# Two of the four weight sums of a pair by adding DMAs instead of VectorE adds

## The chip, the cores and the metric

One core of one Trainium2 chip. The metric is the device time of one execution in microseconds. The text names engines as the profile does: PE is TensorE's matmul queue (PEld its weight loads), DVE is VectorE, ACT is ScalarE, POOL is GpSimd, SP is SyncE.

## The reference

One inference step of a two-layer decoder trunk, on 512 prompt tokens and 8 sample tokens together (T = 520 columns), width 1024, all in float32:

- layer 0: RMSNorm, then retention (4 heads, in chunks of 128) beside a gMLP gating unit (4 groups), one input projection and one output projection
- layer 1: RMSNorm, then a convolution module (gated projection, causal depthwise convolution of width 31, LayerNorm, swish, projection)
- after each: `x = x + square(relu(rmsnorm(x) @ w1)) @ w2` with a hidden width of 4096
- a final RMSNorm; the recurrent and convolution states are outputs too

The change is in the product `rmsnorm(x) @ w1` of both layers.

## The kernel before

Activations lie feature by token: a tile of 128 features has 520 columns, in two halves of 260. A weight unit (1024 rows by 128 output columns) is loaded by `load_w` (line 124, SyncE's queue) as a tile `raw` of 128 x 8 x 128, 512 KB, of which there are four. To keep float32 accuracy, `split` (lines 132 and 133) turns each half unit into a rounded part `wh` (ScalarE) and a rest `wl` (VectorE subtract); there are five such pairs of tiles. Each product is then three matmuls per 128 x 128 block: high by high, low activation by high weight, high activation by low weight.

The first feed-forward product is computed with a seven-product scheme of Strassen's kind (class `Pair`). A pair is two weight units `t` and `b`, each of two halves: `a11`, `a12` from `t`, `a21`, `a22` from `b`. Four sums of halves are formed, each 128 x 512 numbers, 256 KB:

- s1 = a21 + a22 (line 232), s2 = s1 + a11 (line 233), s4 = s2 + a12 (line 234), s3 = a11 + a21 (line 235)

All four are VectorE adds into four tiles of the tag `wsum`. The seven products use a11, a12, s4, a22, s1, s2, s3; each splits its weight and runs 12 matmuls (line 245). `run` calls the products in the order 1, then the product 4 left over from the pair before, then 2, 5, 6, 3, 7; s1 is the weight of product 5, s2 of 6, s4 of 3, s3 of 7. The activations' side of the scheme is prepared by `Tokens.sums` (lines 203 to 214).

The two layers have 29 pairs: in each, 16 double units of `w1`, of which one (layer 0) or two (layer 1) are computed plainly. `ffn` has four blocks; pairs of a block alternate with "down" units, which multiply by `w2`:

```python
            for i in range(KH):
                up(0, i)
            for blk in range(1, 4):
                up(blk, 0)
                down(blk - 1, 0)
                up(blk, 1)
                ...
```

A down unit is 48 matmuls (line 161, tile `y`). Before the first feed-forward stage stands the output projection (tile `ops`), whose sums go into `x` (line 805) and through `Norm.chunk` (lines 357 and 358; its squares are summed by GpSimd, line 374). At the kernel's very start the eight chunks of the input are loaded (SyncE, lines 405 and 410), turned into `n0h` and `n0l` (line 357, 358) and multiplied with the first weight units.

The instructions' order on each engine is not the program's: the kernel is built with `schedule_with_timeline_sim=True`, by a planner that simulates a timeline at build time and lets each engine issue what is ready, earlier lines first. Each engine then works through its queue in order; a tile of a tag can be written when the one that had its place before is released.

Of the kernel before, what the change touches and what calls it, by code (L numbers as in the profile page):

```python
# [6 lines left out]
F32 = mybir.dt.float32  # L7
# [3 lines left out]
ALU = mybir.AluOpType  # L11
# [3 lines left out]
P = 128  # L15
D = 1024
# [60 lines left out]
def trunk_kernel(tc, a, o):  # L77
    nc = tc.nc
    te, ve, se, pe_ = nc.tensor, nc.vector, nc.scalar, nc.gpsimd
    with ExitStack() as st:  # L80
        cp = st.enter_context(tc.tile_pool(name="const", bufs=1))
        big = st.enter_context(tc.tile_pool(name="big", bufs=5))
        wp = st.enter_context(tc.tile_pool(name="w", bufs=3))
# [7 lines left out]
        def open_stage(name):  # L91
            stage.close()
            return stage.enter_context(tc.tile_pool(name=name, bufs=2, reuse_waits="tile"))

        mp = open_stage("mix0")
# [10 lines left out]
        def aux(name):  # L106
            self_n[0] ^= 1
            return ps.tile([P, 512], F32, name=name, tag="auxA" if self_n[0] else "auxB", bufs=2)
# [13 lines left out]
        def load_w(ap, row, col):  # L122
            raw = wp.tile([P, C, P], F32, name="raw", tag="raw", bufs=RAWS)
            nc.sync.dma_start(raw, ap[row // D, col // P])
            return raw

        KH = C // 2
# [93 lines left out]
        class Pair:  # L221
# [5 lines left out]
            def load(self):  # L227
                ap, row, cols = self.src
                t, b = [load_w(ap, row, c) for c in cols]
                a11, a12, a21, a22 = t[:, :KH], t[:, KH:], b[:, :KH], b[:, KH:]  # L230
                s1, s2, s3, s4 = [wp.tile([P, KH, P], F32, name=f"S{i}", tag="wsum", bufs=4) for i in range(4)]
                ve.tensor_add(s1, a21, a22)
                ve.tensor_add(s2, s1, a11)
                ve.tensor_add(s4, s2, a12)
                ve.tensor_add(s3, a11, a21)
                self.w = {1: a11, 2: a12, 3: s4, 4: a22, 5: s1, 6: s2, 7: s3}
                self.banks = [aux("p" + n)[:, :HALF] for n in "pqr"]

# [557 lines left out]
        mp = open_stage("ffn0")  # L796
# [136 lines left out]
        mp = open_stage("mix1")  # L933
# [4 lines left out]
        for c in range(CFULL, C):  # L938
            tag, bufs, parts = (("s0", 3, 1), ("s0", 3, 1), ("s0", 3, 1), ("S", 1, 1))[c - CFULL]
# [175 lines left out]
        mp = open_stage("ffn1")  # L1115
# [72 lines left out]
```

## Time and profile before

| | |
|---|---|
| median of 3 runs | 1317.53 us (1316.22 to 1317.74) |
| profiled execution | 1319.12 us, span 1317.4 us |
| busy: PE / DVE / ACT / POOL | 1273.5 / 923.0 / 648.7 / 242.7 us |
| mean granted clock of TensorE | 0.985 |
| moved by DMA | 149.21 MB, mean 113 GB/s |
| first feed-forward product and down units of layer 0 | about 399 to 752 us |
| of layer 1 | about 943 to 1304 us |

Busy time is the sum of an engine's instructions; a matmul of 260 columns takes 283 ns from start to end in it, but the next one starts before it ends. A row of a group gives line, engine, operation, output tile and inputs, count, busy time, and the idle time before it with what ended it. A row of the timeline gives start, duration, engine, line and tiles. The clock is 1.00 at full speed.

### The profile page before, as it was taken

The numbers are of one execution on the slowest core, as the hardware profiler recorded it, in microseconds if no ns is written. First come the engines' busy times: TensorE is split into PE (matmuls) and PEld (weight loads), VectorE is DVE, ScalarE is ACT, GpSimd is POOL, SyncE is SP. The second block draws the span as 40 slices with busy tenths as digits, with TensorE's granted clock in tenths as the row PEclk, the third lists the DMA queues.
The fourth block names the chain that finished last, engine by engine and source line by source line (L and its number), as shares of the span: only waits on it lengthen the run. The fifth ranks groups of instructions, "written<-read, shape, count | busy, mean of one in ns | idle before, by whom it ended". The sixth has DMA issues, their size and how long they took to land.

```text
span 1317.4 us, 26073 instructions
## 1 busy us (share of the span) xinstructions
PE 1273.5 (97%) x10618; PEld 1241.4 (94%) x10618; DVE 923.0 (70%) x1634; ACT 648.7 (49%) x1160; POOL 242.7 (18%) x226
## 2 busy tenths in 40 slices
PE   9999999799999999999999999989989999999996
PEld 8999999799998999999999998858989999999995
DVE  6833668965688866766755699968997667676544
ACT  7432343433356643544444476547756445454342
POOL 0521013640020000000000469842200000000012
PEclk9999999899999999999999999999989999999998
DMA  7323235773222323332322322453523333332321
GB/s 281 97 86 104 85 130 193 249 278 111 81 82 81 99 94 97 97 113 81 114 96 96 93 85 81 140 129 112 161 65 97 103 90 101 109 97 81 97 81 65
DMA packets 50407, 149.21 MB, mean 113 GB/s; under 512 B 6112, under 2 KB 13280, under 8 KB 50288
## 3 DMA queue, kind: packets, MB, share of 16 engines
q1 hardware_dynamic: 45888, 134.11, 33.1%
q0 software_dynamic: 3456, 12.58, 2.7%
q8 instruction: 83, 1.36, 0.4%
q10 hardware_dynamic: 944, 0.86, 0.2%
q14 instruction: 36, 0.29, 0.1%
HBM read 139.35 MB, written 9.13 MB: 113 GB/s over the span
## 4 chain that ended last, share of the span: by engine, by line
PE 85%; DVE 9%; issue 2%; ACT 2%; DMA 1%; DVEq 0%; SPq 0%
PE y L161 27%; PE in L161 15%; PE pp L245 12%; PE pq L245 6%; PE ci L161 4%; PE ops L161 3%; PE pr L245 3%; PE f L161 3%; PE opr L161 3%; DVE wl L133 2%; PE co L178 2%; DVE cv L1023 2%; PE cvB L993 1%; PE opr L178 1%; ACT wh L132 0%
## 5 line engine op out<-in xcount | busy, mean ns | idle before, releaser
L132 ACT ACTIVATE wh<-raw 128x512 fp32r<-128x512 f32 x403 | 252.3, 629 | 347.2 <-PE in L161 101.9
L133 DVE TENSOR_TENSOR wl<-raw,wh 128x512 fp32r<-128x512 f32 x403 | 301.0, 749 | 165.8 <-ACT wh L132 159.0
L161 PE MATMUL y<-f,wh 128*128 128x260 f32 x2016 | 323.9, 283 | 0.8 <-DVE x L872 0.8
L161 PEld LDWEIGHTS y<-f,wh 128*128 128x128 f32 x2016 | 275.8, 188 | 1.2 <-DVE x L872 1.2
L161 PE MATMUL y<-f,wl 128*128 128x260 f32 x1008 | 202.6, 282 | 0.0
L161 PEld LDWEIGHTS y<-f,wl 128*128 128x128 f32 x1008 | 155.3, 188 | 0.0
L161 PE MATMUL in<-n0h,wh 128*128 128x260 f32 x640 | 133.0, 287 | 1.2 <-DVE k L470 0.8
L161 PE MATMUL in<-n0l,wh 128*128 128x260 f32 x640 | 130.8, 285 | 1.2 <-DVE n0l L358 1.0
L161 PE MATMUL in<-n0h,wl 128*128 128x260 f32 x640 | 129.6, 284 | 0.1
L132 ACT ACTIVATE wh<-S 128x512 fp32r<-128x512 f32 x116 | 73.1, 631 | 91.4 <-PE y L161 45.5
L133 DVE TENSOR_TENSOR wl<-S,wh 128x512 fp32r<-128x512 f32 x116 | 79.3, 687 | 49.6 <-ACT wh L132 48.4
L161 PEld LDWEIGHTS in<-n0h,wh 128*128 128x128 f32 x640 | 99.0, 188 | 3.6 <-PE in L161 1.3
L161 PEld LDWEIGHTS in<-n0l,wh 128*128 128x128 f32 x640 | 98.7, 188 | 2.7 <-DVE n0l L358 2.5
L245 PE MATMUL pp<-Th,wh 128*128 128x260 f32 x348 | 98.3, 283 | 0.9 <-ACT Th L213 0.9
L161 PEld LDWEIGHTS in<-n0h,wl 128*128 128x128 f32 x640 | 98.6, 188 | 0.4 <-DVE wl L133 0.3
L245 PE MATMUL pp<-Tl,wh 128*128 128x260 f32 x348 | 98.1, 282 | 0.0
L245 PE MATMUL pp<-Th,wl 128*128 128x260 f32 x348 | 97.8, 282 | 0.0
L1016 POOL TENSOR_TENSOR pacc<-pacc,pp 128x512 f32<-128x512 f32 x60 | 88.1, 1478 | 4.5 <-ACT pp L1015 1.7
L374 POOL TENSOR_TENSOR n2acc<-n2acc,n2sq 128x520 f32<-128x520 f32 x5 | 7.0, 1402 | 344.9 <-DVE n2l L358 327.3
L374 POOL TENSOR_TENSOR n4acc<-n4acc,n4sq 128x520 f32<-128x520 f32 x5 | 6.5, 1307 | 346.7 <-ACT n4sq L371 346.7
L245 PEld LDWEIGHTS pp<-Th,wh 128*128 128x128 f32 x348 | 65.5, 189 | 1.4 <-ACT Th L213 1.1
L245 PEld LDWEIGHTS pp<-Tl,wh 128*128 128x128 f32 x348 | 65.5, 188 | 0.0
(406 smaller groups left out, 2919.2 us busy)
## 6 DMA issues: line engine op xcount, KB each, us to landing
raw<-in_ffn_w SPq DMA_DIRECT2D x128, 512.0 KB, 3.6
raw<-in_ab_w_in SPq DMA_DIRECT2D x39, 512.0 KB, 3.7
S<-in_state_ret POOLq DMA_DIRECT2D x16, 512.0 KB, 4.8
raw<-in_ab_w_out SPq DMA_DIRECT2D x16, 512.0 KB, 3.7
raw<-in_conv_w_in SPq DMA_DIRECT2D x16, 512.0 KB, 3.7
raw<-in_conv_w_out SPq DMA_DIRECT2D x16, 512.0 KB, 3.7
X<-xscr SPq DMA_DIRECT2D x32, 132.0 KB, 3.3
x<-in_xT SPq DMA_DIRECT2D x16, 260.0 KB, 5.3
```

The source lines that it names most:

```text
L132: se.activation(hi, sp, AF.Copy)
L133: ve.tensor_sub(lo, sp, hi.bitcast(F32))
L161: te.matmul(pts[hf], wt[:, k % KH, :], x(k, SECOND if hf else FIRST)[i == 1], start=k == order[0] and i == 0, stop=k == order[-1] and i == 2)
L178: te.matmul(pt, wt[:, k % KH, :], xt, start=n == 0 and i == 0, stop=n == C - 1 and i == 2)
L245: te.matmul(bank, wt[:, k, :], xt, start=n in (1, 2, 5) and k == 0 and i == 0, stop=k == KH - 1 and i == 2, skip_group_check=True)
L374: eng.tensor_add(self.acc, self.acc, sq)
L993: te.matmul(acc[32 * g:32 * g + 32, :], diag[c, k][:, g, :], X[:, g, k:k + HC], start=k == 0, stop=k == ns - 1)
L1016: pe_.tensor_add(pacc, pacc, pp)
L1023: ve.scalar_tensor_tensor(out=o, in0=win(k), scalar=dw[:, c, k:k + 1], in1=acc, op0=ALU.mult, op1=ALU.add)
```

## The change

s1 and s3 are no longer computed by VectorE. One tile `S31` holds both (two such tiles, in the place of four single ones). GpSimd issues four loads from the weights in device memory for each pair: a22 into s1, a11 into s3, and then, with `accum_op`, a21 added to s1 and a21 added to s3. An adding load waits for the plain load into the same place. s2 and s4 stay VectorE adds, into two tiles of a new tag in the stage's own pool. The tiles `t` and `b` are still loaded whole by SyncE, because products 1, 2 and 4 and the kept adds read them. Per pair, 256 KB each, that is 1 MB of further reads and two VectorE instructions less.

```diff
-                s1, s2, s3, s4 = [wp.tile([P, KH, P], F32, name=f"S{i}", tag="wsum", bufs=4) for i in range(4)]
-                ve.tensor_add(s1, a21, a22)
+                s31 = wp.tile([P, 2, KH, P], F32, name="S31", tag="wsum", bufs=2)
+                s3, s1 = s31[:, 0], s31[:, 1]
+                w1, w2 = [ap[row // D, c // P] for c in cols]
+                nc.gpsimd.dma_start(s1, w2[:, KH:])
+                nc.gpsimd.dma_start(s3, w1[:, :KH])
+                nc.gpsimd.dma_start(s1, w2[:, :KH], accum_op=ALU.add)
+                nc.gpsimd.dma_start(s3, w2[:, :KH], accum_op=ALU.add)
+                s2, s4 = [mp.tile([P, KH, P], F32, name=f"S{i}", tag="wsum24", bufs=2) for i in (2, 4)]
                 ve.tensor_add(s2, s1, a11)
                 ve.tensor_add(s4, s2, a12)
-                ve.tensor_add(s3, a11, a21)
```

## Prediction

> **What bounds the kernel now.** I read the page's engine totals and chain first, then busy time by stretches of 10 us, then the instructions around the stretches in which TensorE is not full.
>
> ```profile
> span 1317.4 us, 26073 instructions
> PE 1273.5 (97%) x10618; PEld 1241.4 (94%) x10618; DVE 923.0 (70%) x1634; ACT 648.7 (49%) x1160; POOL 242.7 (18%) x226
> PE 85%; DVE 9%; issue 2%; ACT 2%; DMA 1%; DVEq 0%; SPq 0%
> 500.00:510.00 10.00, 10.00 (x86) 10.00 (x86) 7.53 (x13) 4.85 (x9) 0.00 (x0) 1.00 0.39 119
> 400.00:410.00 10.00, 7.90 (x55) 6.77 (x53) 9.93 (x20) 5.84 (x13) 0.00 (x0) 1.00 0.01 2
> 410.00:420.00 10.00, 9.16 (x70) 8.55 (x70) 8.52 (x15) 5.79 (x13) 0.00 (x0) 1.00 0.36 106
> 960.00:970.00 10.00, 6.92 (x33) 5.94 (x34) 10.00 (x20) 5.27 (x10) 0.00 (x0) 0.74 0.01 2
> ```
>
> Columns of the stretches: length, then busy time and count of PE, PEld, DVE, ACT, POOL, then clock, DMA share, GB/s. TensorE is the bound. Inside the feed-forward stages (500 to 510 is typical) it runs 86 matmuls in 10 us, 0.116 us each, while VectorE has slack; the weight sums made there cost nothing today. TensorE falls short only where a feed-forward stage begins: 400 to 420 lacks 31+16 matmuls, 5.5 us, and 960 to 970 lacks 53. In both VectorE is full. So the change can gain only there.
>
> **The removed adds.** Minimum, median and maximum in ns:
>
> ```profile
> L232 DVE TENSOR_TENSOR S<-raw x29: 676/692/694, 378.3 to 1228.3; 128x512 f32<-128x512 f32 x29
> L235 DVE TENSOR_TENSOR S<-raw x29: 676/682/685, 383.2 to 1232.0; 128x512 f32<-128x512 f32 x29
> 397.97 0.68 DVE L232 TENSOR_TENSOR S<-raw 128x512 f32<-128x512 f32 x1
> 407.10 0.68 DVE L235 TENSOR_TENSOR S<-raw 128x512 f32<-128x512 f32 x1
> 400.26 0.69 DVE S L233
> 402.19 0.69 DVE S L234
> 943.41 8.37 PE f L161 x68
> 943.78 0.68 DVE L232 TENSOR_TENSOR S<-raw 128x512 f32<-128x512 f32 x1
> 948.48 0.68 DVE L235 TENSOR_TENSOR S<-raw 128x512 f32<-128x512 f32 x1
> ```
>
> VectorE loses 58 instructions, 29x0.692+29x0.682 = 39.8 us. Nearly all of it lies beside a full TensorE and is worth 0. At the first stage's start neither removed add is on the chain (the two rows without an operation are of the chain, and are the kept sums s2 and s4 of the second pair). But those two wait today for an s1 that needs the later of two weight tiles. With s1 loaded long before, they can fill the room that the first pair's removed adds leave, and the chain loses up to 2x0.69 = 1.4 us; the add at 407.10 delays work behind it by up to 0.7. Bounds: 0 to 2.1 gained, and at most the 5.5 us lost there if everything else falls into place. I take 1.3, near the two rows on the chain. At the second stage's start the removed adds (943.78, 948.48) lie in a stretch where the chain is on TensorE, and the hole at 960 comes later and holds no sums: 0, at most 1.4.
>
> **The loads added to the steady stages.** 29x4 = 116 transfers of 256 KB, 30.4 MB, and 116 issues on GpSimd. SyncE's queue issues what it did; scratch sums s2 and s4 only change their tiles.
>
> ```profile
> raw<-in_ffn_w SPq DMA_DIRECT2D x128, 512.0 KB, 3.6
> S<-in_state_ret POOLq DMA_DIRECT2D x16, 512.0 KB, 4.8
> L627 POOL DMA_DIRECT2D S<-in_state_ret x16: 748/758/966, 176.4 to 280.7; - x16
> 287.23 0.75 POOL L647 DMA_DIRECT2D out_ret_s<-S  x1 [5.80 <-DVE S L645]
> 287.35 0.68 DVE L133 TENSOR_TENSOR wl<-raw,wh 128x512 fp32r<-128x512 f32 x1
> 418.12 0.68 DVE L133 TENSOR_TENSOR wl<-S,wh 128x512 fp32r<-128x512 f32 x1
> 436.63 0.69 DVE L233 TENSOR_TENSOR S<-S,raw 128x512 f32<-128x512 f32 x1
>   DVE S L232: 3.5, 10
>   ACT wh L132: 3.8, 5
> ```
>
> An issue costs GpSimd 0.76 us, 88 us in all, in stages where it is idle (0.00 in the stretches above). It doesn't slow VectorE: the add at 287.35 beside the issue at 287.23 took its usual 0.68. No row has an adding load. Its nearest is the plain GpSimd load of twice the size, 4.8 us to landing. An adding load waits on GpSimd for the plain one; queued behind that wait is only the next sum's load, and who waits is VectorE's s2. One pair's chain: four issues 3.0 + two landings 9.6 = 12.6 us; half of that if size rules, double if adding takes three times as long. The sums have two tiles, so a pair's loads start when the pair two before it has split its s3. The tightest case is the first pair of the second block: split ended at 418.8, s2 added at 436.6, 17.8 us later. VectorE may be scheduled to add sooner, as soon as the weight tile is there, and then stand for a few us; TensorE has up to five split halves in hand, 5x12x0.116 = 7 us. I take 0; 2 us if that cover is gone. Where down units lie between pairs there is more time.
>
> The Trainium skill, in DMA: Bandwidth & Descriptors, section Anatomy of one DMA, fits a GpSimd load as 2.0 us plus bytes over 436 GB/s. By it a 512 KB load would take an estimated 3.2 us where the row has 4.8, so here it is short; a pair's chain by it would be 3.0 + 2x2.6 = 8.2 us, an estimate too, hidden like mine.
>
> More traffic for the weight tiles (DMA share 0.39 at 500 to 510): 1 MB per pair beside 1 MB of its own and the down units' tiles. The last two rows are all that was ever waited for a weight tile in the whole run (us, times), 7.3 us, with 3.6 to landing; they are fetched well ahead. 0, at most a few us.
>
> **What the loads do at the kernel's start.** This is the term against the change. Their source is an input and the first two pairs' tiles are free from the beginning, so nothing holds these eight loads back:
>
> ```profile
> 0.81 0.10 POOL L705 MEMSET smv<- 128x2 f32 x1 [0.29 <-POOLq L1169]
> 30.65 1.83 POOL L442 TENSOR_TENSOR cs<-cs,n0r 128x520 f32<-128x520 f32 x1 [29.75 <-DVE n0r L333]
> 16.98 0.57 SPq L269 DMA_DIRECT2D dws<-in_dws  x1
> L944 POOL TENSOR_TENSOR diag<-ids,dws x4: 1917/2362/2371, 744.8 to 751.3; 128x1024 f32<-128x1024 f32 x4
> 5.00:10.00 5.00, 4.25 (x24) 3.17 (x23) 3.64 (x5) 4.61 (x9) 0.00 (x0) 1.00 1.04 391
> 10.00:15.00 5.00, 4.22 (x26) 3.38 (x27) 3.94 (x7) 5.00 (x10) 0.00 (x0) 1.00 1.03 398
> 25.00:30.00 5.00, 5.00 (x41) 4.88 (x40) 2.57 (x6) 2.81 (x6) 0.00 (x0) 1.00 0.55 207
> 1.72 4.45 DMA x<-in_xT
> 6.19 0.73 ACT n0h L357
> 6.92 0.53 ACT n0sq L371
> 7.45 0.62 ACT n0h L357
> ```
>
> The planner issues what is ready: the convolution's taps, first used at 744.8, are loaded at 16.98, and a memset of the gating stage runs at 0.81. GpSimd then has nothing until 30.65. So I expect the first two pairs' plain loads at 0.9 to 4 us and the adding ones behind them. The transfer engines are full from 5 to 15 us (1.04, 1.03), and the chain runs through an input chunk that lands at 6.17. Eight loads are 2.1 MB: 5.3 us of these engines at 395 GB/s, the upper bound. The first is issued by 1.7 us; if the engines serve both queues evenly until 6.2, the chunk loses half of 4.5 us, 2.2. After it ScalarE, at 0.62+0.53 = 1.15 us per chunk, and not DMA sets the pace, which hides the rest. The lower bound is 0 (loads issued late, or served after). I take 2.2.
>
> The Trainium skill, same page, section Queues, rings and completion order, says that each transfer engine goes round its queues packet by packet. By that rule the chunk loses what I took; were the queues served in order of issue, it would lose almost nothing.
>
> **Sum.** The profiled execution took 1319.12 us, 1.7 outside its span. 1319.1 - 1.3 + 2.2 + 0 = 1320.0. It stands 1.6 above the median of the runs, 1317.53, so as a median: 1318.4.
>
> **Rivals.**
>
> (a) The start costs more, through the clock.
>
> ```profile
> 960.00:965.00 5.00, 2.78 (x18) 2.40 (x19) 5.00 (x9) 2.84 (x6) 0.00 (x0) 0.97 0.02 3
> 965.00:970.00 5.00, 4.14 (x17) 3.54 (x17) 5.00 (x12) 2.43 (x4) 0.00 (x0) 0.50 0.00 0
> 970.00:975.00 5.00, 5.00 (x24) 4.78 (x23) 2.98 (x6) 1.70 (x4) 0.00 (x0) 0.50 0.32 105
> ```
>
> After five us with 2.78 of TensorE's work the clock stood at 0.50 for ten. At 5 to 10 us TensorE has 4.25 busy now; 2.2 less is under 2.78, so from a chunk about 1.5 us late it decides. Half speed over some 5 to 10 us costs 2.5 to 5: 1321 to 1323.5, I say 1322. Against it: 400 to 410 had 7.90 of 10 and kept its clock.
>
> (b) The other side, faster: the loads reach the start too late or too thinly to delay the chunk. Then the gain is left: -1.3, to -4 if the freed VectorE time draws more of the 5.5 us together: 1316.2 to 1313.5. For it: the chunk's own queue is far ahead when the first GpSimd load starts.
>
> (c) Adding loads are slow. If a pair's chain passes 17.8 us, VectorE stands at s2 once; past about 30 us it would stand in each of some 25 pairs, at 1 us per us: 40 us of chain gives 1317 + 25x10 = 1567; 32 gives 1367. No row prices it. That sums come late everywhere needs twice my 12.6.
>
> **How the numbers follow.** Forecast 0.42, (a) 0.24, (b) 0.28, (c) 0.06. A measurement of this kernel tells about 0.2%, 2.6 us. Faster by more: half of (b) and a little of the forecast, 0.17. Slower: (a), (c), a tenth of the forecast, 0.33. Same 0.50. Range from (b)'s middle to past (a): 1314 to 1325, leaving (c) and the far end of (b) out; the forecast's own is 1316 to 1321.
>
> **What the profile would show.** L232 and L235 gone, VectorE's busy time near 923-40. GpSimd with loads at 0.9 to 4 us and the input chunk's wait longer than 4.45; if they stand at 370 instead, the start term is wrong. The sums s2 of the second pair before 400, and more than 125 matmuls in 400 to 420. The clock in 10 to 25 us, 1.00 or 0.50, decides (a). VectorE waiting at s2 for a DMA decides (c). 500 to 510 should still hold 86 matmuls; if not, contention that I put at 0 is the error.

## The result and the profile after

The changed kernel takes 1326.26 us (median; 1323.20 to 1328.44), the kernel before 1317.25 us beside it (1316.22 to 1318.54): ratio 1.0072, 95% interval 1.0062 to 1.0083, slower by 9.0 us. The profiled execution took 1325.49 us, 6.4 us more than that of before: the one profiled before stands 1.9 us above the median of the runs beside it, this one 0.8 below its own, so the traces hold 6.4 of the 9.0 us. The page's totals and its chain after the change:

```profile
span 1323.7 us, 26200 instructions
PE 1275.4 (96%) x10618; PEld 1241.4 (94%) x10618; DVE 886.3 (67%) x1576; ACT 649.9 (49%) x1160; POOL 326.3 (25%) x342
PE 81%; DVE 12%; DMA 3%; issue 2%; ACT 1%; DVEq 0%; SPq 0%
```

VectorE lost its 58 adds and 36.7 us of busy time (a moment that two instructions of an engine share counts once in it, so it is less than the sum of their durations). That is not where the time went: the chain's share of DMA has gone from 1% to 3%. Busy time by stretches (the columns are those of the prediction):

```profile
5.00:10.00 5.00, 3.65 (x20) 2.50 (x18) 2.88 (x4) 3.25 (x6) 2.35 (x3) 1.00 1.01 362
10.00:15.00 5.00, 3.24 (x17) 2.21 (x15) 2.73 (x4) 4.08 (x7) 1.14 (x2) 0.95 1.08 269
15.00:20.00 5.00, 4.95 (x17) 3.57 (x17) 2.47 (x5) 1.46 (x2) 0.00 (x0) 0.50 1.09 304
20.00:25.00 5.00, 4.75 (x23) 4.45 (x23) 4.76 (x8) 4.88 (x8) 0.00 (x0) 0.53 1.07 402
400.00:410.00 10.00, 10.00 (x84) 9.94 (x84) 9.06 (x16) 7.99 (x14) 0.34 (x1) 1.00 0.11 40
410.00:420.00 10.00, 9.05 (x70) 8.30 (x69) 9.10 (x18) 6.62 (x15) 2.62 (x4) 1.00 0.68 164
500.00:510.00 10.00, 10.00 (x86) 10.00 (x86) 4.08 (x8) 4.59 (x8) 1.31 (x2) 1.00 0.65 159
965.00:970.00 5.00, 2.05 (x15) 1.71 (x14) 5.00 (x10) 3.43 (x7) 1.17 (x2) 1.00 0.00 0
970.00:975.00 5.00, 4.22 (x22) 4.01 (x22) 5.00 (x12) 1.79 (x3) 1.64 (x2) 0.66 0.56 140
```

Three things are to be seen. Between 10 and 20 us the transfer engines are full but move only 269 and 304 GB/s (before 398 at 10 to 15), and from 14 us on TensorE's clock is 0.50 for ten us. Between 400 and 420 TensorE makes 151 matmuls where it made 125 (the two rows count three twice, those that lie across 410). And 500 to 510 still holds 86.

To place the time, each matmul of a kernel is set beside the matmul of the same tile and rank in the trace of before; the median difference of their starts in a stretch is the lag, in us. The lag at the end is the difference in span.

| stretch of before, us | 22-26 | 300-398 | 418-424 | 600-740 | 880-940 | 950-960 | 980-990 | 1260-1320 |
|---|---|---|---|---|---|---|---|---|
| changed kernel | 7.3 | 5.4 | 2.2 | 4.0 | 5.1 | 6.6 | 4.5 | 6.4 |

So 7.3 us are lost at the start, 3.2 gained where the first feed-forward stage begins, 1.8 lost up to the end of layer 0's, 1.5 at 940 to 950, 2.1 gained where the second stage begins and 1.9 lost in it. Two steps are not the change's: between 200 and 300 us profiled executions differ by about 2 us either way (of the kernels below one loses 0.9 there, another gains 2.6), and the step of 1.1 at 870 also stands in a kernel without one added load. The start, from GpSimd's timeline and the chain:

```profile
1.37 0.73 POOL L234 DMA_DIRECT2D S<-in_ffn_w  x1 [0.47 <-issue]
3.16 0.57 POOL L235 DMA_DIRECT2D S<-in_ffn_w  x1
6.21 0.90 POOL L236 DMA_DIRECT2D S<-in_ffn_w  x1 [2.48 <-DMA S<-in_ffn_w]
10.30 0.87 POOL L237 DMA_DIRECT2D S<-in_ffn_w  x1
1.73 4.52 DMA x<-in_xT
6.26 13.82 DMA raw<-in_ab_w_in
20.11 0.64 ACT wh L132
```

The plain loads go out at 1.4 to 3.2 us, the adding ones at 6.2 to 10.3. The second input chunk is not late (4.52 us, before 4.45). What is late is all behind it, up to the second weight tile, which ScalarE can split at 20.11 us; the adding loads are what runs then. The waits that are new or longer in the feed-forward stages (us in total, times, longest), VectorE's and then TensorE's weight loader's; before, VectorE stood 3.5 us in all for weight tiles, at the old s1, and the loader 1.5 us in two waits at `f` and none at `y`:

```profile
DVE S L239 <- DMA raw<-in_ffn_w: 33.8, 11, 4.1
DVE S L239 <- DMA S<-in_ffn_w: 6.7, 2, 3.5
PEld f L161 <- DVE wl L133: 4.5, 3, 3.1
PEld y L161 <- DVE wl L133: 2.6, 5, 0.8
```

Of the 4.5 us at `f`, 3.9 stand behind 960 us, where VectorE is full. L239 is the sum s2. It stands eleven times for the pair's first weight tile and twice for the sum's own loads. The instance at 421.91 shows the harm: for 2.8 us nothing behind s2 on VectorE runs, and the split at 424.67, for which TensorE then waits 0.39 us, stands behind it. The instance at 454.20 is one of the two for the sum's loads; TensorE's wait at 457.70 follows from it in the same way. At 949.96 TensorE waits for an `x` (L1094) that stands on VectorE behind s2 (945.11) and s4 (948.13), which here wait for no transfer.

```profile
418.42 0.68 DVE L133 TENSOR_TENSOR wl<-S,wh 128x512 fp32r<-128x512 f32 x1
421.91 0.69 DVE L239 TENSOR_TENSOR S<-S,raw 128x512 f32<-128x512 f32 x1 [2.81 <-DMA raw<-in_ffn_w]
424.67 1.28 DVE L133 TENSOR_TENSOR wl<-raw,wh 128x512 fp32r<-128x512 f32 x2
425.41 0.51 PE L161 MATMUL f<-n1h,wl 128*128 128x260 f32 x2 [0.39 <-DVE wl L133]
454.20 0.69 DVE L239 TENSOR_TENSOR S<-S,raw 128x512 f32<-128x512 f32 x1 [3.27 <-DMA S<-in_ffn_w]
457.70 0.51 PE L161 MATMUL y<-f,wl 128*128 128x260 f32 x2 [0.38 <-DVE wl L133]
949.96 0.47 PE L161 MATMUL f<-n3h,wh 128*128 128x260 f32 x2 [1.73 <-DVE x L1094]
```

The lag rises in steps behind these waits: by 0.6 us behind the one at 421.91, by 0.6 and 0.8 behind the two for the sums' loads (454.20 and 1006.10), and by 0.2 to 0.7 behind four more of those for weight tiles. So of the 3.7 us lost inside the two stages some 2.3 go with late weight tiles and some 1.4 with late sums. The 1.5 at 940 to 950 go with the wait at 949.96; the kernels below in which s2 and s4 come later do not have this step.

### The profile page after: what moved, and what is told of

It reads as the page before. It is cut to its first block, busy times and chain, and to the rows that moved or that the text cites. A ratio compares the mean times of both kernels' runs of the same rounds, so it can differ in the third digit from the quotient of the medians.

```text
span 1323.7 us, 26200 instructions
## 1 busy us (share of the span) xinstructions
PE 1275.4 (96%) x10618; PEld 1241.4 (94%) x10618; DVE 886.3 (67%) x1576; ACT 649.9 (49%) x1160; POOL 326.3 (25%) x342
## 4 chain that ended last, share of the span: by engine, by line
PE 81%; DVE 12%; DMA 3%; issue 2%; ACT 1%; DVEq 0%; SPq 0%
PE y L161 27%; PE in L161 16%; PE pp L250 11%; PE pq L250 5%; PE pr L250 3%; DVE wl L133 3%; PE co L178 3%; PE ci L161 3%; PE opr L161 3%; PE ops L161 3%; DVE cv L1028 2%; PE f L161 2%; DMA raw<-in_ffn_w 1%; DMA raw<-in_ab_w_in 1%; PE cvB L998 1%
## 5 line engine op out<-in xcount | busy, mean ns | idle before, releaser
L234 POOL DMA_DIRECT2D S<-in_ffn_w x29 | 16.7, 576 | 425.1 <-DVE wl L133 424.6
L833 ACT ACTIVATE f<-f 128x520 fp32r<-128x520 f32 x58 | 37.0, 638 | 63.6 <-DVE f L832 63.5
L250 PEld LDWEIGHTS pp<-Th,wl 128*128 128x128 f32 x348 | 65.3, 188 | 0.0
```

The source lines that it names most:

```text
L234: nc.gpsimd.dma_start(s1, w2[:, KH:])
L250: te.matmul(bank, wt[:, k, :], xt, start=n in (1, 2, 5) and k == 0 and i == 0, stop=k == KH - 1 and i == 2, skip_group_check=True)
L833: se.activation(dst[:, 0, u], src, AF.Square)
```

## The experiments

The theory: the loss has two causes that are independent of each other, (1) the early loads, above all the adding ones, starve the kernel's first 20 us, and (2) s2, which now needs only the loaded s1 and the first weight tile, is queued on VectorE ahead of that tile's landing. The rivals: the halved clock for (1), slow adding loads for (2). Each kernel ran in turn with the kernel before; ratios are to it, with 95% intervals. In the first edit all first loads are "held"; several of the later kernels keep it.

**All eight first loads held.** `last_hist` is GpSimd's last multiply of the convolution history, `held` counts pairs:

```diff
+                hold = tc.issue_after(last_hist.ins) if len(held) < 2 else nullcontext()
+                held.append(self)
+                with hold:
                     nc.gpsimd.dma_start(s1, w2[:, KH:])
                     ...
```

> The eight GpSimd loads of the first two pairs of layer 0 are held behind GpSimd's last multiply of the convolution history (about 333 us), so none runs at the start; everything else as in the changed kernel. Theory S (the early loads cost 5.4 to 7.3 us at the start): 1326.3 - 5.4 to 7.3 = 1319.0 to 1320.9; the clock stays at 1.00 in 10 to 25 us; the second pair's sums are still in time near 400. Rival (the start's delay is made up later, since the lag fell from 7 to 5.4 us by 260): 1324 or more.

Measured: 1316.60 us (1315.04 to 1319.39), ratio 1.0000 (0.9990 to 1.0011). The start's loss is gone, and all of it stays gone: the lag is -0.6 at 25 us and -1.3 at 398. The time is 2.4 us under the expectation's low end: of the 9.7 us that it is faster than the changed kernel the start makes 7.9 by the lags, and the rest is smaller losses behind it (0.9 us of the loader's waits in down units instead of 2.6). Why those are smaller is open. The stretches:

```profile
10.00:15.00 5.00, 4.27 (x29) 3.44 (x29) 4.22 (x7) 5.00 (x10) 0.00 (x0) 1.00 1.03 409
15.00:20.00 5.00, 5.00 (x44) 5.00 (x43) 4.93 (x9) 4.36 (x8) 0.00 (x0) 1.00 0.98 317
```

**Only the adding loads held.**

```diff
                 nc.gpsimd.dma_start(s1, w2[:, KH:])
                 nc.gpsimd.dma_start(s3, w1[:, :KH])
+                with hold:
                     nc.gpsimd.dma_start(s1, w2[:, :KH], accum_op=ALU.add)
                     ...
```

> Only the adding loads of the first two pairs are held until about 333 us; their four plain loads stay at 1 to 3 us. Theory SA (the adding loads are what starves the start): within 1 us of the kernel with all eight held, 1319 to 1321. Rival SB (any early load takes its bytes' share: half the bytes, half the delay): 2.7 to 3.6 us above that kernel, 1322 to 1324.

Measured: 1320.15 us (1317.31 to 1323.27), ratio 1.0023 (1.0011 to 1.0034): 3.5 us above the kernel with all held, as SB said (its 1322 to 1324 took that kernel for slower than it is). The lag at 25 us is 2.6 us: four plain loads are 1.05 MB, 2.6 us of the engines at 400 GB/s, so they cost about what their bytes take. The clock was halved here too, from 8 to 15 us, but the chain does not lead over TensorE then: it goes from the fourth input chunk, which lands at 10.85 us, through ScalarE and VectorE to the matmuls at 16.42:

```profile
5.00:10.00 5.00, 3.29 (x15) 2.39 (x14) 2.12 (x3) 2.42 (x6) 0.00 (x0) 0.81 0.98 336
10.00:15.00 5.00, 5.00 (x20) 4.16 (x20) 3.44 (x5) 4.73 (x10) 0.00 (x0) 0.51 1.05 410
2.67 8.18 DMA x<-in_xT
16.42 7.66 PE in L161 x60
```

**The first two pairs' adding loads overwrite, and nothing is held.**

```diff
+                how = dict(accum_op=ALU.add) if len(held) > 1 else {}
+                held.append(self)
-                nc.gpsimd.dma_start(s1, w2[:, :KH], accum_op=ALU.add)
+                nc.gpsimd.dma_start(s1, w2[:, :KH], **how)
                 ... (s3 likewise)
```

> The changed kernel with its eight early loads, but the four adding ones of the first two pairs overwrite instead of adding (these two pairs' s1 and s3 lack an addend); same bytes, same issues, the other 27 pairs unchanged. Theory A (the adding costs the engines about twice the time per byte at the start): the lag at 25 us is near 5 us, between the 2.6 us with four plain loads and the 7.3 us with four plain and four adding, and the time 1323 to 1324.5. Rival B (only the bytes count, and their number makes the rest): lag 7 us, 1325.5 to 1327.

Measured: 1322.52 us (1321.14 to 1325.10) beside 1316.09, ratio 1.0057 (1.0043 to 1.0071). The time is under both expectations, in a turn in which the kernel before took less time too; by the ratio (1.0057 of 1317.25 is 1324.8) it stands between them. The lag at 25 us decides for A: 4.4 us. Four plain loads make 2.6, four more plain ones 1.8, but four adding ones in their place 4.7 (7.3 - 2.6). The engines' rate at 10 to 15 us agrees with A, 399 GB/s here against 269:

```profile
10.00:15.00 5.00, 4.89 (x19) 3.94 (x18) 3.18 (x5) 4.51 (x9) 0.65 (x2) 0.52 1.04 399
```

**The changed kernel with a filled start**: one matmul into an unused bank behind each of the first seven chunks of the first unit.

```diff
+                if fill and n < C - 1:
+                    with tc.issue_after(m.ins):
+                        for _ in range(fill):
+                            te.matmul(busy[:, :P], ones, ones, start=True, stop=True)
```

> The changed kernel with its early loads, and one extra 128x128 matmul into an unused bank behind each of the first unit's seven first chunks, so that TensorE is not idle enough for the clock to be halved at 14 us. Theory C (the halved clock is what makes the start dear): the lag at 25 us falls from 7.3 us to 3 or less and the time to about 1322. Rival D (late input chunks and the late second weight tile, 6.4 us later than before, make the lag by themselves, and the halved clock lies inside their delay): lag 6 to 7 us, 1325 to 1327.

Measured: 1325.74 us (1323.17 to 1328.08), ratio 1.0063 (1.0051 to 1.0075). The clock stays at 1.00, and the lag at 25 us is 6.65 instead of 7.3. So without the halved clock 0.7 us is gained, net of the added matmuls and of a second weight tile that landed 0.3 us later in this execution (20.40 instead of 20.08 us); by itself the halved clock was worth about 1 us, an estimate from these numbers. Most of it lay inside the delay of the transfers. The kernel with late s2 and s4 alone, below, starts with the same loads: there the clock was halved at another time (0.50 at 10 to 15 us, 0.99 at 15 to 20), and the lag is 7.8.

```profile
10.00:15.00 5.00, 3.21 (x18) 2.42 (x19) 2.38 (x4) 3.22 (x6) 1.54 (x2) 1.00 1.10 282
15.00:20.00 5.00, 3.94 (x24) 2.96 (x23) 1.93 (x3) 2.52 (x4) 0.00 (x0) 1.00 1.08 306
6.03 14.37 DMA raw<-in_ab_w_in
```

**All first loads held, and every adding load overwrites.**

```diff
-                    nc.gpsimd.dma_start(s1, w2[:, :KH], accum_op=ALU.add)
+                    nc.gpsimd.dma_start(s1, w2[:, :KH])
                     ... (s3 likewise)
```

> As the kernel with all eight first loads held, but the adding loads overwrite instead of adding, in all 29 pairs (s1 and s3 lack one addend); same bytes, same issues. Theory PA (adding loads are slow and take engine time from the weight tiles, which is the 3 to 4 us lost in the steady feed-forward stages): at least 2 us below that kernel, the sum loads land in 3 to 4 us. Rival PB (VectorE stands at s2 because s2 is queued before its weight tile has landed, whatever the sums cost): within 1 us of that kernel, and VectorE still waits some 25 us at s2 for the weight tiles.

Measured: 1312.89 us (1311.14 to 1314.88), ratio 0.9970 (0.9957 to 0.9983): 3.7 us below the kernel with all held, as PA said. But VectorE still waits at s2 for the weight tile, as PB said:

```profile
DVE S L242 <- DMA raw<-in_ffn_w: 25.7, 14, 3.2
PEld y L161 <- DVE wl L133: 0.6, 1, 0.6
L239 POOL DMA_DIRECT2D S<-in_ffn_w x29: 537/537/546, 334.3 to 1190.7; - x29
DMA to landing us min/median/max: 2.8/5.0/6.1
```

The waits remain but are shorter (3.2 at the longest, 4.3 in the kernel with all held), and TensorE's split halves in hand cover them. PA's 3 to 4 us to landing hold for the first loads alone (2.9 and 3.2 in the median): the second ones, in the adding loads' place (L239 and L240 here), land in 5.0 and 5.6 though they add nothing. Neither theory fits alone: the adding loads make the weight tiles later (median to landing 3.7 us here, 4.2 with adding), and s2's place in the queue passes the lateness on.

**All first loads held, and s2 and s4 behind the split of product 1.** `last_lo` is VectorE's subtract of that split:

```diff
+            def sums24(self):
+                ...
+                with tc.issue_after(last_lo[0].ins):
+                    ve.tensor_add(s2, self.w[5], self.w[1])
+                    ve.tensor_add(s4, s2, self.w[2])
             def product(self, n):
                 hi, lo = split(self.w[n])
+                if n == 1:
+                    self.sums24()
```

> As the kernel with all eight first loads held, but VectorE's sums s2 and s4 are issued behind the split of the pair's first product, which needs the same weight tile. Theory PB (the wait at s2 for the weight tile stands ahead of other VectorE work): the 33.8 us of waits at s2 for weight tiles vanish and the time is 2 to 4 us below that kernel, 1316 to 1319. Rival PA (slow adding loads): within 1 us of that kernel, 1319 to 1321.

Measured: 1312.33 us (1311.73 to 1313.23), ratio 0.9963 (0.9949 to 0.9977), 4.3 us below the kernel with all held, 4.8 faster than before and 13.9 faster than the changed kernel, with all adding loads in. There is no wait at s2 for a DMA any more, and no wait of the loader for a split in a down unit; the lag between 424 and 740 us stays at -5.4 where it rose by 1.2 in the changed kernel. So the order is what the loss needed, as PB says: with the queue in this order no cost of the slow adding loads shows. Of the 3.7 us between the two profiled executions the lags put 2.1 behind 398 us and 1.6 before it, where the two kernels do the same.

```profile
400.00:410.00 10.00, 8.38 (x63) 7.50 (x61) 9.98 (x19) 5.84 (x12) 2.95 (x4) 1.00 0.57 128
410.00:420.00 10.00, 10.00 (x86) 10.00 (x85) 8.52 (x16) 7.99 (x16) 2.92 (x4) 1.00 0.65 199
```

**The same edit alone, on the changed kernel, nothing held.**

> The changed kernel with its eight early loads, with only s2 and s4 moved behind the split of the first product. Theory I (the two losses are independent): 1326.3 - 4.3 = 1322, with the lag of 7 us at the start and none added in the feed-forward stages. Rival J (they share a cause): 1324 or more, or under 1319.

Measured: 1319.59 us (1315.72 to 1320.58) beside 1316.09, ratio 1.0021 (1.0009 to 1.0032). The lag is 7.8 at 25 us, 4.3 all the way from 424 to 740, and -0.1 from 980 to the end. So the start's loss is there in full and the steady loss is gone, as I says. The total stands between I and J (1.0021 of 1317.25 is 1320.0), 2 us lower than I put it, and the second stage's beginning gains 4.1. By the ratios the late s2 and s4 are worth 0.0051 here and 0.0037 with the loads held, the same within the intervals: independent, as far as these runs tell.

**The kernel before with its four adds behind the split of product 1.**

```diff
+                with tc.issue_after(last_lo[0].ins):
+                    ve.tensor_add(s1, a21, a22)
+                    ve.tensor_add(s2, s1, a11)
+                    ve.tensor_add(s4, s2, a12)
+                    ve.tensor_add(s3, a11, a21)
```

> The kernel before, all four sums still made by VectorE, with one edit: they are issued behind the split of the pair's first product. Theory V (what the repaired change gains over before, 4.8 us, comes from VectorE having two adds less per pair): this stays at before's time or above it, 1316 to 1320, since the first sum is then later. Rival O (the gain comes from the order alone, adds that no longer stand ahead of splits): about 1312 to 1313.

Measured: 1314.95 us (1313.46 to 1318.30), ratio 0.9984 (0.9974 to 0.9993), between the two: the order alone gains 2.2 us, and the two adds made by DMA the other 2.6 of the 4.8 (a split that is rough, since the intervals of 0.9984 and 0.9963 still touch). This kernel's profiled execution stands 3.3 us over its median; its lag is 0.8 at 398 and -1.1 at the end, with +1.1 at 870, where no load of sums exists.

**Where the loads are worth it.** Three more, each made from the kernel with all first loads held and late s2 and s4. First, only s1 by DMA, s3 again an add:

```diff
-                    nc.gpsimd.dma_start(s3, w1[:, :KH])
-                    nc.gpsimd.dma_start(s3, w2[:, :KH], accum_op=ALU.add)
+                    ve.tensor_add(s3, self.w[1], self.w[0])
```

> As the kernel whose sums s2 and s4 stand behind the first split, but only s1 is made by DMA; s3 is VectorE's again, behind s4. Half the added traffic, one add more per pair. Theory T (traffic still costs something there): below 1312.3, to 1310. Rival F (VectorE's free time at the stage's start is what counts): 1313 to 1315.

Measured: 1315.42 us (1312.07 to 1316.88), ratio 0.9985 (0.9976 to 0.9994): as F says, 0.4 us above its range. Half the traffic less does not make up for one add more per pair, so no cost of the traffic shows. Second, only the first two pairs of each layer by DMA:

```diff
+                self.first = sum(p.src[0] is ap for p in held) < 2
+                if self.first:
                     ... (the four loads)
+                        if not self.first:
+                            ve.tensor_add(self.w[5], self.w[0], self.w[4])
                         ... (s2, s4; s3 like s1)
```

> As the kernel whose first loads are held and whose s2 and s4 stand behind the first split, but only the first two pairs of each layer have sums made by loads; the other 25 pairs have all four sums by VectorE, behind the first split. Theory T (the gain is made only where the stages begin): within 1.5 us of that kernel, 1311 to 1314. Rival V (the freed VectorE time counts in the steady stages too): 1314.5 or more.

Measured: 1312.88 us (1309.48 to 1314.08) beside 1316.09, ratio 0.9976 (0.9967 to 0.9985). In microseconds as T says; by the ratio it is between T and V, and its interval overlaps that of 0.9963. The lag falls by 2.5 and 3.6 us at the two stages' beginnings and by nothing elsewhere. Third, on the kernel that has all pairs' s1 and s3 by DMA, s2 and s4 of each layer's first pair by seven loads more, instead of two adds:

```diff
+                for s, parts in zip(self.s24, ((a22, a21, a11), (a22, a21, a11, a12))):  # as slices of w2, w1
+                    for i, part in enumerate(parts):
+                        nc.gpsimd.dma_start(s, part, **(dict(accum_op=ALU.add) if i else {}))
```

> As the kernel whose first loads are held and whose s2 and s4 stand behind the first split, with one thing added: in the first pair of each layer s2 and s4 are made by adding loads too (three and four loads). Theory T (VectorE bounds the stage's start, so two adds less there gain again): 1 to 2 us below it, 1310.5 to 1311.5. Rival G (GpSimd, waiting for seven loads in a row, brings the norm's sums late, or the sums come late): 1312.3 or more.

Measured: 1311.02 us (1310.43 to 1312.24) beside 1316.09, ratio 0.9965 (0.9953 to 0.9978): the same as without them (0.9963). In microseconds that is T, by the ratio G's price. Neither of G's reasons shows in its trace: GpSimd alone waits for these loads, and each of its sums for the norm still waits for ScalarE's squares, not for a load. The stretch 400 to 420 holds 145 matmuls, 146 with the adds of that pair (the rows further up count three twice) and 145 with the second variant; so those two adds seem no longer to be what bound it.

**Who issues the plain loads**: SyncE instead of GpSimd, in the kernel with all first loads held and late s2 and s4.

```diff
-                    nc.gpsimd.dma_start(s1, w2[:, KH:])
+                    nc.sync.dma_start(s1, w2[:, KH:])
                     ... (s3 likewise)
```

> As the kernel whose sums s2 and s4 stand behind the first split, but the plain loads are issued by SyncE, between its weight tiles, and only the adding ones by GpSimd; SyncE's loads of the first two pairs follow its second load of the convolution history. Theory Q (an adding load's cost lies in the adding, not in who issues the plain load): within 1 us, 1311.5 to 1313.5. Rival W (SyncE's queue then holds weight tiles behind a sum load that waits for its tile): 1315 or more, with VectorE or ScalarE waiting on weight tiles.

Measured: 1312.69 us (1311.17 to 1314.06), ratio 0.9963 (0.9951 to 0.9975): Q, no difference.

The lags of these kernels side by side, as above:

| kernel | 22-26 | 300-398 | 418-424 | 600-740 | 950-960 | 980-990 | end |
|---|---|---|---|---|---|---|---|
| changed | 7.3 | 5.4 | 2.2 | 4.0 | 6.6 | 4.5 | 6.4 |
| adding loads held | 2.6 | 0.0 | -3.2 | -2.7 | 0.0 | -0.5 | 0.3 |
| all held | -0.6 | -1.3 | -4.5 | -3.4 | -1.2 | -4.1 | -3.1 |
| all held, all plain | -0.5 | -2.4 | -5.6 | -5.5 | -4.4 | -7.3 | -6.6 |
| all held, late s2, s4 | -0.3 | -2.9 | -5.4 | -5.4 | -4.5 | -6.9 | -6.8 |
| late s2, s4 alone | 7.8 | 6.8 | 4.3 | 4.3 | 4.0 | -0.1 | -0.1 |
| first two pairs of a layer | -0.3 | -0.1 | -2.6 | -2.6 | -2.5 | -6.1 | -6.1 |

## Why the prediction was wrong, by its steps

It put the profiled execution at 1320.0 and the median at 1318.4, at most 1325; they are 1325.49 and 1326.26. By the lags the terms that follow miss the profiled execution by +5.1 (start), +5.2 (inside the stages and at 940 to 950) and -4.0 (transitions); -0.8 is not the change's. The median's further 2.4 us come from the step that took 1.6 off for a profiled execution above its median: this one stood 0.8 below.

- **The start (+2.2): the cause right, the steps to the number wrong; it was +7.3.** The loads went out where they were expected and took the engines from the input. But the chunk that the term is worked out on was late by 0.07 us, not 2.2 (its wait went from 4.45 to 4.52), and with the adding loads held by 1.35 (ScalarE takes it up at 7.54 instead of 6.19). That the plain loads alone cost 2.6 is near 2.2 by luck: there the fourth chunk, 2.4 us late, set it, and ScalarE's pace did hide the rest. The step that failed is "After it ScalarE ... and not DMA sets the pace, which hides the rest". In the changed kernel ScalarE then stands for five more chunks and for the second weight tile, and the adding loads run beside exactly these: 4.7 us more. The upper bound of 5.3, eight loads at 395 GB/s, took an adding load's bytes at a plain load's rate; with eight plain loads the lag is 4.4, within it.
- **Rival (a), the clock**: it was halved for about 10 us, as foreseen, but the filled start shows it worth 0.7 us, or about 1. Its forecast of 1322 came from a halved clock on a TensorE with work to do; here TensorE mostly waited for data. Rival (b)'s gain did not come even without the early loads: with all of them held the ratio is 1.0000, because the stages lose what their beginnings gain.
- **The steady stages (0): wrong, the fallback was nearer.** The text had the event ("VectorE may be scheduled to add sooner ... and then stand for a few us") and its price ("2 us if that cover is gone"), and took the cover for granted. The loader's waits for splits in down units are 2.6 us, none in the kernels with late s2; the lag puts 1.8 and 1.9 us inside the two stages and 1.5 at 940 to 950, where s2 and s4 stand ahead of the `x` that TensorE needs. The reason given, that weight tiles "are fetched well ahead", was read from a kernel in which no add stood in front of them: the old s1 needed the second tile of the pair, and with it in the queue VectorE waited 3.5 us in all. The stretch 500 to 510 holds its 86 matmuls; it was too short a sample to show a loss spread over 700 us.
- **The transitions (-1.3 and 0): right in sign, too small.** -3.2 and -2.1. The freed VectorE time drew more of the first stage's missing 5.5 us together than the chain's two rows said; and the second stage, put at 0 because its removed adds lay where TensorE ran the chain, gained all the same. (VectorE, said to be full in 400 to 420, had 8.52 us of the second ten.) 151 matmuls in 400 to 420 answer the "more than 125".
- **Rival (c), slow adding loads**: an adding load lands in 7.6 us where the same load without adding takes 5.0 and a first load 3.0, but the sums were late only twice, 6.7 us of VectorE's time and some 1.4 of the kernel's. The chain's estimate of 12.6 us held by luck: first loads were cheaper than taken and adding ones dearer. What did not hold is the room of 17.8 us, read from the old order. In the old kernel the pair that adds its s2 at 457.72 had it too; in the changed one VectorE has come to this s2 by 450.93, 7.8 us after the pair's first load went out (443.09), and stands until 454.20. Of the pair whose loads begin at 496.39 the last load goes out at 500.59; with the median of 8.1 us to landing for that line, s3 is there 12.3 us after the first issue.

```profile
496.39 0.57 POOL L234 DMA_DIRECT2D S<-in_ffn_w  x1 [16.30 <-DVE wl L133]
500.59 0.86 POOL L237 DMA_DIRECT2D S<-in_ffn_w  x1
L237 POOL DMA_DIRECT2D S<-in_ffn_w x29: 849/946/1259, 8.0 to 1204.7; - x29
DMA to landing us min/median/max: 4.5/8.1/10.2
```

The sum of the lags: 7.3 - 1.9 (before 398 us, not the change's) - 3.2 + 1.8 + 1.1 (at 870, not the change's) + 1.5 - 2.1 + 1.9 = 6.4.

## What to carry to other kernels

A load with no predecessor is put at the kernel's start; price it there against the bytes that the start is waiting for, or give it an edge to a later instruction of its engine (here that edge alone was worth 9.7 us). When an operation loses one of its inputs, look at what else it waits for: it may now be queued ahead of a transfer that its old place hid, so tie it behind something that needs the same transfer. In this kernel moving work to DMA paid only at the two places where VectorE bounds, and two pairs of each layer were enough to have most of it.

## What the runs showed of the hardware

**An adding load takes about twice the engines' time of a plain one.** Median to landing and the issue's duration, for 256 KB (minimum, median, maximum in ns and us), in the changed kernel; the software queue's row of the page for the kernel with all held, then for the same with every load plain, then for the kernel whose plain loads SyncE issues:

```profile
L234 POOL DMA_DIRECT2D S<-in_ffn_w x29: 564/568/726, 1.4 to 1200.6; - x29
DMA to landing us min/median/max: 2.8/3.0/6.5
L236 POOL DMA_DIRECT2D S<-in_ffn_w x29: 850/883/912, 6.2 to 1203.7; - x29
DMA to landing us min/median/max: 3.8/7.6/8.7
q0 software_dynamic: 16448, 43.00, 13.2%
q0 software_dynamic: 12736, 43.00, 9.6%
q0 software_dynamic: 11808, 27.79, 9.7%
```

Between the first two rows of the queue: same bytes, 3.6% more of 16 engines' span, and 3712 more packets, 64 for each of the 58 adding loads. In the kernel before the queue's 12.58 MB took 2.7%, so that 30.4 MB of plain loads took 6.9%, half of them 3.45%; the adding half took 3.45 + 3.6 = 7.05%, 2.0 times as much. The last row, with the adding half alone in this queue, gives 9.7 - 2.7 = 7.0%. The time to landing overstates it: of the 7.6 us against 3.0 a part is the place, since with all first loads held the same second load lands in 7.5 with adding and in 5.0 without. The Trainium skill, in Collectives: The Full Stack, section The bandwidth ceiling, says of a reduce-scatter's transfers that the add itself costs nothing but needs two source reads and so two descriptors per chunk, which halves the rate (1.93 measured there); the 2.0 agrees, and the packets of a load go from 80 to 144. The Trainium skill, in DMA: Bandwidth & Descriptors, section Anatomy of one DMA, gives a fit by which 256 KB would land in an estimated 2.6 us: near the first load's 3.0, short of the 5.0 of a plain load in the second place, and far from the adding one's 7.6.

**TensorE's busy share does not tell alone when the clock is halved.** With 3.24 of 5 us busy at 10 to 15 us the clock went to 0.50 at 14 us in the changed kernel; with 3.21 busy in the same stretch it stayed at 1.00 in the filled start. From 12 to 14 us it was 1.35 of 2 us busy in the one and only 1.03 in the other. What the difference was is open.
